# A GLA state update computed by pairs of sequences, two 64-row products side by side

## The chip, the cores and the metric

The kernel runs on one core of one Trainium2 chip. A core has a matrix engine (PE, with its weight loads listed apart as PEld), a vector engine (DVE), a scalar engine (ACT), a general engine (POOL) and an engine that mostly issues transfers (SP). They run their own instruction streams in order and wait for one another by semaphores. The metric is the device time of one execution in microseconds; lower is better.

## The reference

One step of a decoder layer: a Mamba-2 (SSD) branch and a gated linear attention (GLA) branch, merged by gates, then cross-attention and a convolutional feed-forward block, for a prompt of 256 tokens and, with the same weights, for 8 sample sequences of 4 tokens each. The change touches the sample part of the GLA branch, which has 4 heads with keys of 256 and values of 512:

```python
def step(S, inp):                       # here a chunk is the 4 tokens of a sample
    qc, kc, vc, gc = inp
    b = jnp.cumsum(gc, axis=1)
    qe = qc * jnp.exp(b)
    ke = kc * jnp.exp(-b)
    att = jnp.where(mask, jnp.einsum('bihk,bjhk->bhij', qe, ke), 0.0)
    o = jnp.einsum('bhij,bjhv->bihv', att, vc) + jnp.einsum('bihk,bhkv->bihv', qe, S)
    last = b[:, -1]
    S = jnp.exp(last)[..., None] * S + jnp.einsum('bjhk,bjhv->bhkv', kc * jnp.exp(last[:, None] - b), vc)
    return S, o
```

For each of 8 sequences and 4 heads, a state S of 256 x 512 floats is read from memory, used for the output, decayed, given a product of 4 tokens' keys and values, and written back.

## The kernel before

Everything is laid out with features on the 128 partitions and the 288 tokens (256 of the prompt, 32 of the samples) along the free axis. The bulk is projections (`proj_w`): a weight tile is loaded, split into a rounded high part (`whi`, ACT, L103) and the remainder (`wlo`, DVE, L105), and multiplied as high x high (L147), high x low (L148) and low x high (L151), 288 columns a matmul, in the format fp32r. The split tiles live in rings of five (`WB`). The products of the `mem` projections (L315, L316, L319) are the same with 512 columns.

Scans are generators that are woven into the projections: `weave` runs the projections of the next unit and the output projection of the last one as the main stream, and advances the scan by a share at each step. A `yield` is one such share, and `yield 1.25` counts as more. The final order on each engine is made by a scheduler that simulates a timeline; transfers marked `keep_in_program_order` keep their order. Four SSD units are followed by four GLA units, one for each head.

In a GLA unit (`gla_scan`, L1035) the 32 sample tokens are repeated four times down the partitions (`rep4`, L639), so that rows 0-31, 32-63, 64-95 and 96-127 hold the same tokens. `stack_r` (L646) gives the four groups of rows of `vst` the values' high, low, high, low parts, and `stack_l` (L657) gives `kst` and `atsl` the keys' high, high, low, low parts. One 128-row product of the two thus sums all four combinations, which restores nearly full precision.

The states come four ahead through POOL's queue (`load_state`, L1040), into six buffers of the tag `c4`. Then, for each half q of the sequences: eight products of queries and states for the output (L1150), each 32 columns wide, so that four of them lie in different column strips of the array; then for each sequence b a copy of `kst` masked to b's rows (`kb`, L1156), two products of 128 rows x 512 columns (L1159), each into its own bank of the three that `mm_tile` has, and two updates of the state on DVE (L1160). The state is stored through SP's queue (L1163), which also carries the weights, and the load of b + 4 follows.

The loop as it is before:

```python
for b in range(4 * q, 4 * q + 4):
    sin = sins[b]
    kb = pa.tile([P, 256], F32R, tag="kb", bufs=2, name="kb")
    V.tensor_scalar(kb, kst, bmask[:, b:b + 1], None, ALU.mult)
    for k in range(2):
        a = mm_tile()
        MM(a, kb[:, k * P:(k + 1) * P], vst, start=True, stop=True)
        V.scalar_tensor_tensor(sin[:, k, :], ...)
        yield 1.25
```

Other places named below: L566 is a small product of 32 rows in the set-up of the SSD branch; L870 is a product of the SSD scan that is 32 columns wide; L821, L823 and L825 are SSD products 64 columns wide; L398 and L469 are small DVE operations of the set-up.

Of the kernel before, what the change touches and what calls it, by code (L numbers as in the profile page):

```python
# [8 lines left out]
F32 = mybir.dt.float32  # L9
F32R = mybir.dt.float32r  # L10
# [6 lines left out]
P = 128  # L17
# [3 lines left out]
NB = 8  # L21
# [21 lines left out]
def hybrid_step(ctx: ExitStack, tc: tile.TileContext, I: dict, O: list):  # L43
# [185 lines left out]
    smask4 = p1.tile([P, NS], F32, name="smask4")  # L229
    smaski = p1.tile([P, NS], I32, name="smaski")  # L230
    bmask = p1.tile([P, NB], F32, name="bmask")
    rm_g = p1.tile([P, T], F32, name="rm_g")

    def starts(rm, c):
# [31 lines left out]
    with pool("p0") as p0:  # L266
# [194 lines left out]
        for c in range(4):  # L461
# [7 lines left out]
        V.tensor_copy(smaski, smask4)  # L469
# [169 lines left out]
    def rep4(src, name):  # L639
# [3 lines left out]
        V.tensor_copy(o, src.unsqueeze(2).to_broadcast([P, n, 4, NS]))  # L643
        return o.rearrange("p t r s -> p t (r s)")

    def stack_r(dst, src):  # L646

        S.copy(dst, src)
        for q in (1, 3):
            rows = slice(q * NS, (q + 1) * NS)  # L650
            V.tensor_tensor(dst[rows], src[rows], dst[rows], ALU.subtract)

    def own(a, q):

        return bass.AP(a.tensor, a.offset + 16 * q, [list(a.ap[0]), [P, 4], [NS + NL, 4], [1, NL]])

    def stack_l(dst, src):  # L657

# [376 lines left out]
    def gla_scan(h, eb, qe, ke, kd, kde, vT, sr):  # L1035

        sq = pa.tile([P, T], F32, tag="sq", bufs=1, name="sqa")
        sins = []

        def load_state(b):  # L1040
            sin = c4([P, 2, 512], "sin")
            tc.keep_in_program_order(G.dma_start(out=sin, in_=I["state_gla"][b, h].rearrange("(k p) v -> p k v", p=P)))
            sins.append(sin)
# [9 lines left out]
        vsr = rep4(vT[:, :, SEQ:T], "vsr")  # L1053
        ksr = rep4(kd[:, :, SEQ:T], "ksr")
        ker = rep4(ke[:, :, SEQ:T], "ker")

        vt = []
        for i in range(2):
            a = mm_tile()
            for t in range(4):  # L1060
                TR(a[:, t * P:(t + 1) * P], vT[:, t, i * P:(i + 1) * P], ident)
            v = b2("vt")
            S.copy(v, a)
            vt.append(v)
            yield

        a = mm_tile()
        for i, (t0, n) in enumerate(TOK):
            for k in range(2):
                MM(a[:, t0:t0 + n], ke[:, k, t0:t0 + n] if i < 2 else ker[:, k, :], qe[:, k, t0:t0 + n],  # L1070
                   start=(k == 0), stop=(k == 1))
        for i in range(2):
            for k in range(2):
                MM(a[:, 288 + 64 * i:352 + 64 * i], kd[:, k, P * i:P * i + P], qe[:, k, P * i + 64:P * i + P],
                   start=(k == 0), stop=(k == 1))
        V.copy_predicated(att, gmask.unsqueeze(1).to_broadcast([P, 2, P]),
                          a[:, 0:SEQ].rearrange("p (c n) -> p c n", n=P))
        V.copy_predicated(ats, smaski, a[:, SEQ:T])
        for rows, op in ((slice(0, P), None), (slice(2 * NS, P), ALU.subtract)):
            f, g = atsl[rows], ats[rows].rearrange("p (q j l) -> p q j l", j=4, l=NL)  # L1080
            f = bass.AP(f.tensor, f.offset, [list(f.ap[0]), [16, 2], [NS + NL, 4], [1, NL]])
            if op is None:
                S.copy(f, g)
            else:
                V.tensor_tensor(f, g, f, op)
        S.copy(att[0:64, :, 64:P], a[0:64, 288:416].rearrange("p (c n) -> p c n", n=64))
        for i in range(2):
            for k in range(2):
                V.tensor_copy(kd[:, k, P * i:P * i + 64], kde[:, k, i, :])
        yield  # L1090

        kt = b2("kt").rearrange("p (c k) -> p c k", k=256)
        a = mm_tile()
        for i in range(2):
            for k in range(2):
                TR(a[:, i * 256 + k * P:i * 256 + (k + 1) * P], kd[:, k, i * P:(i + 1) * P], ident)
        S.copy(kt.rearrange("p c k -> p (c k)"), a)
        yield
        a = mm_tile()
        for t in range(4):  # L1100
            TR(a[:, t * P:(t + 1) * P], vsr[:, t, :], ident)
        vst = r2("vst")
        stack_r(vst, a)
        yield
        a = mm_tile()
        for k in range(2):
            TR(a[:, k * P:(k + 1) * P], ksr[:, k, :], ident)
        kst = pa.tile([P, 256], F32R, tag="kst", bufs=1, name="kst")
        stack_l(kst, a[:, 0:256])
        for k in range(2):  # L1110
            diag(qdm[:, k], qe[:, k, SEQ:T])
        yield

        elp = pa.tile([P, 2], F32, tag="elp", bufs=1, name="elp")
        V.tensor_tensor(elp, eb[:, :, 191], eb[:, :, 255], ALU.mult)
        for k in range(2):
            V.tensor_scalar(qe[:, k, 192:256], qe[:, k, 192:256], eb[:, k, 191:192], None, ALU.mult)
        sprev = None
        for i in range(2):
            sn = c4([P, 2, 512], "sn")  # L1120
            for k in range(2):
                a = mm_tile()
                MM(a, kt[:, i, k * P:(k + 1) * P], vt[i], start=True, stop=True)  # L1123
                if i == 0:
                    S.copy(sn[:, k, :], a)
                else:
                    V.scalar_tensor_tensor(sn[:, k, :], sprev[:, k, :], elp[:, k:k + 1], a, ALU.mult, ALU.add)
                yield
            o = mm_tile()
            for t in range(4):  # L1130
                MM(o[:, t * P:(t + 1) * P], vt[i][:, t * P:(t + 1) * P], att[:, i, :], start=True, stop=(i == 0))
                if i == 1:
                    for k in range(2):
                        MM(o[:, t * P:(t + 1) * P], sprev[:, k, t * P:(t + 1) * P], qe[:, k, P:SEQ], start=False,
                           stop=(k == 1))
            evac(o, i * P, P)
            yield
            sprev = sn
        nc.sync.dma_start(out=o_pgla[0, h].rearrange("(k p) v -> p k v", p=P), in_=sprev)
        for b in range(4):  # L1140
            load_state(b)
        yield

        osa = la_tile()
        MM(osa, atsl, vst, start=True, stop=False)
        for q in range(2):
            for k in (1, 0):
                for j in (3, 2, 1, 0):
                    b = 4 * q + j
                    MM(osa[NS * j:NS * j + NS, :], qdm[:, k, b, :], sins[b][:, k, :], start=False,  # L1150
                       stop=(q == 1 and k == 0))
            yield
            for b in range(4 * q, 4 * q + 4):
                sin = sins[b]
                kb = pa.tile([P, 256], F32R, tag="kb", bufs=2, name="kb")
                V.tensor_scalar(kb, kst, bmask[:, b:b + 1], None, ALU.mult)  # L1156
                for k in range(2):
                    a = mm_tile()
                    MM(a, kb[:, k * P:(k + 1) * P], vst, start=True, stop=True)  # L1159
                    V.scalar_tensor_tensor(sin[:, k, :], sin[:, k, :], eb[:, k, SEQ + 4 * b + 3:SEQ + 4 * b + 4], a,  # L1160
                                           ALU.mult, ALU.add)
                    yield 1.25
                nc.sync.dma_start(out=o_sgla[b, h].rearrange("(k p) v -> p k v", p=P), in_=sin)  # L1163
                if b + 4 < NB:
                    load_state(b + 4)
            if h == 3 and q == 0:
                yield 3
        os_ = b2("os")
        S.copy(os_, osa)
        yield  # L1170
        a = mm_tile()
        for t in range(4):
            TR(a[:, t * P:(t + 1) * P], os_[:, t * P:(t + 1) * P], ident)
        ot = pa.tile([P, P], F32, tag="cst", bufs=2, name="ot")
        for q in range(2):
            S.copy(ot.rearrange("p (t q j l) -> p q t j l", t=4, q=2, j=4)[:, q], own(a, q))
        evac(ot, SEQ, NS)
        yield
        yield
        yield from finish(sr, sq, rg, False)  # L1180
# [650 lines left out]
```

## Time and profile before

| | us |
|---|---|
| median of 3 runs | 2519.35 |
| lowest and highest | 2517.22, 2526.04 |
| the profiled execution, its own time | 2522.44 |
| its span, first to last instruction | 2520.7 |
| state products L1159, first to last start | 771.6 to 1163.7 |

The page's second part shows the span in 40 slices. PE stands at 9 tenths or more nearly throughout, the granted clock at 9 or more in every slice, and the DMA engines between 5 and 8 tenths:

```profile
PE   9999999999999999999999999999999999999998
DVE  6656777796867666666666677567777677676765
PEclk9999999999999999999999999999999999999999
DMA  8776587767868675867778599655555555555553
```

A row of a timeline gives the start in us, the length in us, the engine, the line of the kernel, the operation, the tiles (out<-in), for PE the part of the array that the instruction uses (rows*columns, 128*128 being all of it), the shape and the count. A matmul's length is modelled and overlaps that of the next; its start is recorded. One fp32 matmul shows as two records (two passes), one fp32r matmul as one.

### The profile page before, as it was taken

The numbers are of one execution on the slowest core, as the hardware profiler recorded it, in microseconds if no ns is written. First come the engines' busy times: TensorE is split into PE (matmuls) and PEld (weight loads), VectorE is DVE, ScalarE is ACT, GpSimd is POOL, SyncE is SP. The second block draws the span as 40 slices with busy tenths as digits, with TensorE's granted clock in tenths as the row PEclk, the third lists the DMA queues.
The fourth block names the chain that finished last, engine by engine and source line by source line (L and its number), as shares of the span: only waits on it lengthen the run. The fifth ranks groups of instructions, "written<-read, shape, count | busy, mean of one in ns | idle before, by whom it ended". The sixth has DMA issues, their size and how long they took to land.

```text
span 2520.7 us, 50431 instructions
## 1 busy us (share of the span) xinstructions
PE 2502.4 (99%) x18914; PEld 2411.9 (96%) x18914; DVE 1753.1 (70%) x3752; ACT 1346.9 (53%) x2736; POOL 392.8 (16%) x729
## 2 busy tenths in 40 slices
PE   9999999999999999999999999999999999999998
PEld 8889999998999999999999989999999999999998
DVE  6656777796867666666666677567777677676765
ACT  7655647655463655454445544555555455454545
POOL 3002133342300010000001122402111001020010
PEclk9999999999999999999999999999999999999999
DMA  8776587767868675867778599655555555555553
GB/s 268 221 218 196 171 251 210 228 196 210 245 188 275 183 251 175 248 207 263 202 224 267 180 327 323 213 159 178 170 171 173 170 168 171 170 175 169 168 171 129
DMA packets 442021, 521.95 MB, mean 207 GB/s; under 512 B 26876, under 2 KB 390236, under 8 KB 441712
## 3 DMA queue, kind: packets, MB, share of 16 engines
q1 hardware_dynamic: 407728, 422.34, 54.3%
q0 software_dynamic: 34016, 96.38, 12.0%
q8 instruction: 148, 2.42, 0.4%
q14 instruction: 97, 0.79, 0.1%
q10 hardware_dynamic: 32, 0.01, 0.0%
HBM read 473.13 MB, written 45.48 MB: 206 GB/s over the span
## 4 chain that ended last, share of the span: by engine, by line
PE 95%; DMA 2%; DVE 1%; ACT 1%; issue 0%; POOL 0%; DVEq 0%; ACTq 0%; POOLq 0%
PE acc L148 27%; PE acc L147 27%; PE acc L151 26%; PE acc L315 2%; PE acc L316 2%; PE acc L319 2%; PE la L1541 1%; PE mm L1159 1%; PE la L1150 1%; DMA sqr<-in_state_ssd_dram 1%; PE la L1483 1%; PE mm L1123 1%; DMA sin<-in_state_ssd_dram 1%; DMA raw<-in_w_gla_out_dram 0%; POOL sqr L731 0%
## 5 line engine op out<-in xcount | busy, mean ns | idle before, releaser
L103 ACT CAST whi<-raw 128x512 fp32r<-128x512 f32 x1464 | 897.3, 618 | 1011.9 <-PE acc L148 783.6
L105 DVE TENSOR_TENSOR wlo<-raw,whi 128x512 fp32r<-128x512 f32 x1464 | 997.2, 687 | 607.9 <-ACT whi L103 590.5
L147 PE MATMUL acc<-xn,whi 128*128 128x288 f32 (+1 forms) x1936 | 550.2, 299 | 0.0
L148 PE MATMUL acc<-xn,whi 128*128 128x288 f32 (+1 forms) x1936 | 542.0, 296 | 0.0
L151 PE MATMUL acc<-xn,wlo 128*128 128x288 f32 (+1 forms) x1936 | 414.3, 295 | 0.0
L148 PE MATMUL acc<-hf,whi 128*128 128x288 f32 x1408 | 393.2, 295 | 0.0
L147 PE MATMUL acc<-hf,whi 128*128 128x288 f32 x1408 | 389.0, 292 | 0.0
L147 PEld LDWEIGHTS acc<-xn,whi 128*128 128x128 f32 (+1 forms) x1936 | 364.4, 188 | 9.9 <-issue 7.5
L148 PEld LDWEIGHTS acc<-xn,whi 128*128 128x128 f32 (+1 forms) x1936 | 364.5, 188 | 6.6 <-issue 4.6
L151 PEld LDWEIGHTS acc<-xn,wlo 128*128 128x128 f32 (+1 forms) x1936 | 310.5, 188 | 1.6 <-issue 1.3
L151 PE MATMUL acc<-hf,wlo 128*128 128x288 f32 x1408 | 294.5, 290 | 0.0
L148 PEld LDWEIGHTS acc<-hf,whi 128*128 128x128 f32 x1408 | 264.5, 188 | 0.1
L147 PEld LDWEIGHTS acc<-hf,whi 128*128 128x128 f32 x1408 | 264.0, 188 | 0.1
L151 PEld LDWEIGHTS acc<-hf,wlo 128*128 128x128 f32 x1408 | 226.3, 188 | 0.0
L148 PE MATMUL acc<-pr,whi 128*128 128x288 f32 x704 | 196.6, 295 | 0.0
L147 PE MATMUL acc<-pr,whi 128*128 128x288 f32 x704 | 195.0, 293 | 0.0
L151 PE MATMUL acc<-pr,wlo 128*128 128x288 f32 x704 | 147.4, 290 | 0.0
L147 PE MATMUL acc<-un,whi 128*128 128x288 f32 x512 | 145.3, 300 | 1.2 <-DVE mb L961 0.8
L148 PE MATMUL acc<-un,whi 128*128 128x288 f32 x512 | 143.0, 295 | 0.0
L1655 POOL COPY fsp<-fst 128x16 f32<-128x16 f32 x88 | 37.1, 424 | 656.5 <-DVE av L1667 422.0
L148 PEld LDWEIGHTS acc<-pr,whi 128*128 128x128 f32 x704 | 132.3, 188 | 0.0
L147 PEld LDWEIGHTS acc<-pr,whi 128*128 128x128 f32 x704 | 132.0, 188 | 0.0
(516 smaller groups left out, 4283.4 us busy)
## 6 DMA issues: line engine op xcount, KB each, us to landing
raw<-in_w_in_dram SPq DMA_DIRECT2D x240, 512.0 KB
raw<-in_w_up_dram SPq DMA_DIRECT2D x176, 512.0 KB
raw<-in_w_down_dram SPq DMA_DIRECT2D x88, 512.0 KB
raw<-in_w_cv_dram SPq DMA_DIRECT2D x32, 512.0 KB
raw<-in_w_ssd_out_dram SPq DMA_DIRECT2D x32, 512.0 KB
sin<-in_state_gla_dram POOLq DMA_DIRECT2D x32, 512.0 KB, 5.6
out_dram<-sin SPq DMA_DIRECT2D x32, 512.0 KB
raw<-in_w_gla_out_dram SPq DMA_DIRECT2D x32, 512.0 KB
```

What stands on the lines that cost most here:

```text
L103: S.copy(hi, raw)
L105: V.tensor_tensor(lo, raw, hi, ALU.subtract)
L147: MM(a, hi[:, k, cs], xh, start=(k0 + s0 + k == 0), stop=False)
L148: MM(a, hi[:, k, cs], xl, start=False, stop=False)
L151: MM(a, lo[:, k, cs], xh, start=False, stop=(k0 + s0 + k == nk - 1))
L315: MM(accs[m], mn_hi[:, kk, ms_], hi[:, 0, :], start=(kk == 0), stop=False)
L316: MM(accs[m], mn_lo[:, kk, ms_], hi[:, 0, :], start=False, stop=False)
L319: MM(accs[m], mn_hi[:, kk, ms_], lo[:, 0, :], start=False, stop=(kk == KT - 1))
L1123: MM(a, kt[:, i, k * P:(k + 1) * P], vt[i], start=True, stop=True)
L1150: MM(osa[NS * j:NS * j + NS, :], qdm[:, k, b, :], sins[b][:, k, :], start=False, stop=(q == 1 and k == 0))
L1159: MM(a, kb[:, k * P:(k + 1) * P], vst, start=True, stop=True)
L1655: G.tensor_copy(sp[:, :, 0:2], st.rearrange("p (b k) -> p b k", k=2))
```

## The change

Sequences are handled in pairs (b, b + 4). The rows of the repeated tokens are regrouped by halves: partitions 0-63 hold the 16 tokens of sequences 0-3 four times, partitions 64-127 those of sequences 4-7 (`rep16`, two copies in place of one). High and low parts are made over all rows at once: `stack` computes sign x source on ACT and low x source - that on DVE, with columns `signs` and `lows` of per-row constants (+1 and 1 where the row is to hold the low part, -1 and 0 where the high part). In the set-up these constants and a mask for pairs (`bpair`) are derived from a matrix `sub`, made by two operations on POOL and reduced on DVE.

The masked keys `kb` are made once for a pair. Each of the two sequences takes one half of the rows: two products of 64 rows x 512 columns, the first on partitions 0-63 and the second on 64-127, into two banks. The array fields of these instructions are 64*128, at rows 0 and 64. Then both states are updated. States are loaded in the order 0, 4, 1, 5, 2, 6, 3, 7; both states of a pair are stored together, and the next two loads follow.

```diff
+    def rep16(src, name):
+        n = src.shape[1]
+        o = b2(name).rearrange("p (t f r s) -> p f t r s", f=2, r=4, s=16)[:, :, 0:n]
+        for f in range(2):
+            V.tensor_copy(o[:, f], src[:, :, 16 * f:16 * f + 16].unsqueeze(2).to_broadcast([P, n, 4, 16]))
+        return o.rearrange("p f t r s -> p t f (r s)")
+
+    def stack(dst, src, w):
+        S.activation(dst, src, ACT.Identity, scale=signs[:, w:w + 1])
+        V.scalar_tensor_tensor(dst, src, lows[:, w:w + 1], dst, ALU.mult, ALU.subtract)
...
-        for rows, op in ((slice(0, P), None), (slice(2 * NS, P), ALU.subtract)):
...
+        atp = pa.tile([P, NS], F32R, tag="atp", bufs=1, name="atp")
+        stack(atp, ats, 1)
+        for f in range(2):
+            S.copy(bass.AP(atsl.tensor, atsl.offset + 80 * f, ...), atp[:, 16 * f:16 * f + 16]...)
...
-        stack_r(vst, a)
+        stack(vst, a, 0)
...
-        stack_l(kst, a[:, 0:256])
+        stack(kst, a[:, 0:256], 1)
...
-        for b in range(4):
+        for b in (0, 4, 1, 5):
             load_state(b)
...
-                    b = 4 * q + j
+                    b = 4 * (j // 2) + 2 * q + j % 2
                     MM(osa[NS * j:NS * j + NS, :], qdm[:, k, b, :], sins[b][:, k, :], start=False,
...
-            for b in range(4 * q, 4 * q + 4):
-                sin = sins[b]
+            for j in (2 * q, 2 * q + 1):
                 kb = pa.tile([P, 256], F32R, tag="kb", bufs=2, name="kb")
-                V.tensor_scalar(kb, kst, bmask[:, b:b + 1], None, ALU.mult)
+                V.tensor_scalar(kb, kst, bpair[:, j:j + 1], None, ALU.mult)
                 for k in range(2):
-                    a = mm_tile()
-                    MM(a, kb[:, k * P:(k + 1) * P], vst, start=True, stop=True)
-                    V.scalar_tensor_tensor(sin[:, k, :], sin[:, k, :], eb[...], a, ALU.mult, ALU.add)
-                    yield 1.25
-                nc.sync.dma_start(out=o_sgla[b, h]..., in_=sin)
-                if b + 4 < NB:
-                    load_state(b + 4)
+                    au = [mm_tile() for _ in range(2)]
+                    for f in range(2):
+                        rows = slice(64 * f, 64 * f + 64)
+                        MM(au[f], kb[rows, k * P:(k + 1) * P], vst[rows], start=True, stop=True)
+                    for f in range(2):
+                        b, sin = j + 4 * f, sins[j + 4 * f]
+                        V.scalar_tensor_tensor(sin[:, k, :], sin[:, k, :], eb[...], au[f], ALU.mult, ALU.add)
+                    yield 2.5
+                for b in (j, j + 4):
+                    nc.sync.dma_start(out=o_sgla[b, h]..., in_=sins[b])
+                    if j + 2 < 4:
+                        load_state(b + 2)
...
-        for q in range(2):
-            S.copy(ot...[:, q], own(a, q))
+        for f in range(2):
+            for q in range(2):
+                S.copy(ot...[:, f, q], own2(a, f, q))
```

More of the change, by code (lines that the diff above doesn't have):

```diff
@@ L231, in hybrid_step @@
     bmask = p1.tile([P, NB], F32, name="bmask")
+    half_ = p1.tile([P, 8], F32, name="half_")
+    bpair, lows, signs = half_[:, 0:4], half_[:, 4:6], half_[:, 6:8]
     rm_g = p1.tile([P, T], F32, name="rm_g")
@@ L468, in hybrid_step @@
                             channel_multiplier=-1)
-        V.tensor_copy(smaski, smask4)
+        sub = p0.tile([P, NS, NL], F32, name="sub")
+        G.affine_select(sub, ones.rearrange("p (x l) -> p x l", l=NL), pattern=[[4, NS], [1, NL]], compare_op=ALU.is_ge,
+                        fill=0.0, base=0, channel_multiplier=-1)
+        G.affine_select(sub, sub, pattern=[[-4, NS], [0, NL]], compare_op=ALU.is_ge, fill=0.0, base=0, channel_multiplier=1)
+        smg = p0.tile([P, 2, 16], F32, name="smg")
+        V.tensor_reduce(smg, sub.rearrange("p (f r j) l -> p f (j l) r", f=2, r=4), axis=AX.X, op=ALU.add)
+        V.tensor_copy(smaski, smg.rearrange("p f x -> p (f x)"))
+        last = smg.rearrange("p f (j l) -> p f j l", l=NL)[:, :, :, NL - 1]
+        V.tensor_tensor(bpair, last[:, 0], last[:, 1], ALU.add)
+        own4 = sub[:, :, NL - 1]
+        odd = p0.tile([P, 4], F32, name="odd")
+        for w, v in enumerate((own4.rearrange("p (a r j) -> p r a j", r=2, j=4)[:, 1],
+                               own4.rearrange("p (a r j) -> p r a j", r=2, j=8)[:, 1])):
+            V.tensor_reduce(odd[:, 0:v.shape[1]], v, axis=AX.X, op=ALU.add)
+            V.tensor_reduce(lows[:, w:w + 1], odd[:, 0:v.shape[1]], axis=AX.X, op=ALU.add)
+        V.tensor_scalar(signs, lows, 2.0, -1.0, ALU.mult, ALU.add)
         gm_f = p0.tile([P, P], F32, name="gm_f")
```

35 lines of the change are left out of this document (16 added, 19 removed).

## The prediction

> **What bounds the kernel now.** I read the page first, busy times and the chain that ended last.
>
> ```profile
> PE 2502.4 (99%) x18914; PEld 2411.9 (96%) x18914; DVE 1753.1 (70%) x3752; ACT 1346.9 (53%) x2736; POOL 392.8 (16%) x729
> PE 95%; DMA 2%; DVE 1%; ACT 1%; issue 0%; POOL 0%; DVEq 0%; ACTq 0%; POOLq 0%
> ```
>
> PE, the matrix engine, sets the time. A busy PE says little here, since ends of matmuls are modelled; so from here on I use starts only, and the distance from one start to the next. The changed code runs inside the four GLA scans, between 724 and 1182 us. Busy time of each engine in that stretch, and the chain cut to it:
>
> ```profile
> 724.00:1182.00 458.00, 458.00 (x3401) 433.76 (x3401) 306.34 (x610) 233.43 (x420) 31.77 (x49) 1.00 0.72 226
> by line: PE acc L148 27.1%; PE acc L147 27.1%; PE acc L151 26.7%; PE mm L1159 3.3%; PE la L1150 3.2%; PE mm L1123 3.0%; PE mm L1134 1.6%; PE mm L1131 1.6%; PE mm L1070 1.1%; PE mm L1074 0.8%; PE mm L1061 0.8%; issue 0.5%; PE mm L1096 0.4%;
> ```
>
> Columns of the first row: the stretch, its length, busy us of PE, PEld (weight loads), DVE, ACT, POOL, granted clock, DMA share, GB/s. The clock is full, DVE works 67% and ACT 51%, and hardly anything but matmuls is on the chain. So the change is worth what it does to PE's own sequence; the state product (L1159) holds 3.3% of 458 us, 15.1 us over 64 products, 0.236 us each.
>
> **What one state product costs now.** The group, then PE's order of work around one product, then the same neighbours without one:
>
> ```profile
> L1159 PE MATMUL mm<-vst,kb x64: 389/398/403, 771.6 to 1163.7; 128*128 128x512 f32 x64
> ...
> 771.29 0.43 PE L151 MATMUL acc<-un,wlo 128*128 128x288 f32 x2
> 771.55 0.40 PE L1159 MATMUL mm<-vst,kb 128*128 128x512 f32 x1
> 771.79 0.30 PE L147 MATMUL acc<-un,whi 128*128 128x288 f32 x1
> 771.93 0.30 PE L148 MATMUL acc<-un,whi 128*128 128x288 f32 x1
> ...
> 768.93 0.42 PE L151 MATMUL acc<-un,wlo 128*128 128x288 f32 x2
> 769.18 0.29 PE L147 MATMUL acc<-un,whi 128*128 128x288 f32 x1
> 769.31 0.29 PE L148 MATMUL acc<-un,whi 128*128 128x288 f32 x1
> ```
>
> From the L151 pair to L148 it is 0.64 us with a product and 0.38 without: 0.26. The chain gives 0.236. I take 0.25 us a product, **0.50 for two**. Note the field 128*128: all of these use the array undivided.
>
> **What the change puts in its place.** Two products of 64 rows each, field 64*128, into two PSUM banks. The trace has no such form. It has others that divide the array, and they show the same thing at their edges. Nearest is L566, divided by rows (32*128), between undivided 512-column products; PE first, then its weight loads:
>
> ```profile
> 153.64 0.40 PE L315 MATMUL acc<-whi,mn_hi 128*128 128x512 f32 x1
> 153.87 0.39 PE L316 MATMUL acc<-whi,mn_lo 128*128 128x512 f32 x1
> 154.10 0.63 PE L319 MATMUL acc<-wlo,mn_hi 128*128 128x512 f32 x2
> 154.66 0.48 PE L566 MATMUL mm<-elm,hsel 32*128 32x128 f32 x2
> 155.07 0.50 PE L315 MATMUL acc<-whi,mn_hi 128*128 128x512 f32 x1
> 155.41 0.39 PE L316 MATMUL acc<-whi,mn_lo 128*128 128x512 f32 x1
> ...
> 154.66 0.29 PEld L566 LDWEIGHTS mm<-elm,hsel 32*128 32x128 f32 x2 [0.37 <-PE acc L316]
> 155.07 0.19 PEld L315 LDWEIGHTS acc<-whi,mn_hi 128*128 128x128 f32 x1
> 155.18 0.19 PEld L316 LDWEIGHTS acc<-whi,mn_lo 128*128 128x128 f32 x1
> ```
>
> Plain products follow each other in 0.23 (153.64, 153.87, 154.10). Entry: two L319 should take 0.46 and take 0.56, so 0.10 extra. Inside: 0.41 to the next L315, of which the two passes stream 2 x 0.107 (from the next fence). The other 0.20 is a weight load that hides behind nothing (0.11, as 155.07 to 155.18 shows for one of 128 columns) and 0.09 of emptying. Exit: L315 to L316 takes 0.34 instead of 0.23, another bare load, 0.11. Normally a load starts one matmul ahead; at a change of division it starts with its own matmul. Together **0.10 + 0.20 + 0.11 = 0.41 us for one island** in undivided work.
>
> The second form is four column strips: L1150, and L870 as a short island:
>
> ```profile
> 766.44 1.92 PE L1150 MATMUL la<-sin,qdm 128*32 128x512 f32 x16
> ...
> 766.89 0.13 PEld L1150 LDWEIGHTS la<-sin,qdm 128*32 128x32 f32 x4 [0.30 <-issue]
> 767.32 0.13 PEld L1150 LDWEIGHTS la<-sin,qdm 128*32 128x32 f32 x4 [0.30 <-issue]
> ...
> 363.05 0.41 PE L151 MATMUL acc<-xn,wlo 128*128 128x288 f32 x2
> 363.40 0.63 PE L870 MATMUL mm<-xds,mss 128*32 128x256 f32 x4
> 363.95 0.40 PE L147 MATMUL acc<-xn,whi 128*128 128x288 f32 x1
> 364.19 0.29 PE L148 MATMUL acc<-xn,whi 128*128 128x288 f32 x1
> ```
>
> L1150: sixteen 512-column passes of 0.59 in 1.92 us, four at a time, a round every 0.43 us (0.107 per 128 columns): different strips do run side by side. L870: 1.14 us over neighbours that take 0.38, so 0.76, less two rounds of 256 columns (0.43): 0.33, the same toll with loads of 32 columns for 128.
>
> Now the new island. Streaming 512 columns in fp32r lies between 0.215 (half the fp32 round) and 0.23 (plain spacing): 0.22. The second half starts 0.01 later (four loads within 0.13). So **a pair side by side costs 0.41 + 0.22 + 0.01 = 0.64 us against 0.50 before: +0.14**. A half that stands alone pays the whole toll: 0.63 against 0.25, +0.38. In the order in which the changed program is built, 27 of the 32 pairs are adjacent and 5 are torn apart (the last pair of the first three heads, two in the last head), with L147/L148/L151 between. Sum: 27 x 0.14 + 10 x 0.38 = 3.8 + 3.8 = **+7.6 us**.
>
> Bounds, since rows as strips beside each other are not in this trace: if the second load waits for the first, +0.11 per pair (27 x 0.11 = 3.0 more); if the second product streams only after the first, +0.22 per pair (5.9 more); if a division by 64 rows pays no toll, a pair costs 0.26, that is 27 x -0.24 = -6.5 and nothing for single halves. I take the toll because both divisions shown, by rows and by columns, pay it, and side by side because the column strips do.
>
> The row first: L566 loses 0.10 going in and 0.09 going out beside its bare loads. The Trainium skill, "TensorEngine Tiling (Array Packing)", Key Properties, says why: a change of tiling mode, not of tile alone, drains the engine. The trace agrees with it. The same page's Theoretical Speedup gives up to 2x for 64 rows; by that figure alone, without the drain, 32 pairs would save 32 x 0.24 = 7.7 us, and the change would pay.
>
> **The other edits, off PE's path.** DVE rows by shape for this stretch:
>
> ```profile
> L1160 DVE SCALAR_TENSOR_TENSOR sin<-sin,eb,mm 128x512 f32<-128x512 f32 x64 | 47.6, 745 | 27.3 <-PE mm L1159 26.7
> L1156 DVE TENSOR_SCALAR kb<-kst,bmask 128x256 fp32r<-128x256 f32 x32 | 10.8, 348 | 0.3
> L651 DVE TENSOR_TENSOR vst<-mm,vst 32x512 fp32r<-32x512 f32 x8 | 5.5, 690 | 0.6 <-ACT vst L648 0.3
> ```
>
> Per head DVE loses four masks (4 x 0.35) and two partial subtractions (2 x 0.69), and gains one full-height multiply-subtract of 512 (0.75, as L1160, also out of PSUM); a half-height one of 256 becomes a full-height one, and three repeats become six of half the size. That is 1 to 2 us a head less, on an engine 67% busy: 0. ACT gets four more small copies a head, on an engine 51% busy: 0. Two updates now come back to back, 1.5 us in which no wlo is made; PE holds five split weight tiles (WB) of twelve 0.13 us matmuls, 7.8 us. Without that cover it would cost 0.75 per pair. The set-up has two more POOL masks and seven more small DVE operations, which fall here:
>
> ```profile
> 30.93 0.16 DVE L398 TENSOR_REDUCE mrs<-mss 128x2 f32<-128x8 f32 x1 [0.88 <-ACT junk L347]
> 31.44 1.90 DVE L105 TENSOR_TENSOR wlo<-raw,whi 128x512 fp32r<-128x512 f32 x3 [0.35 <-ACT whi L103]
> ```
>
> At 0.16 each that is 1.1 us, into 1.23 us of idle time: 0, and at most 1.1 were they all in the way and the weight ring empty.
>
> The stores of b and b+4 now stand together, and the last two state loads on POOL's queue wait for both. PE's second group of L1150 waits for those loads, and everything on PE queues behind it. In the tightest head, the last, then in the first; then the last head's busy times, and the load's row of the page:
>
> ```profile
> 1130.30 0.38 SPq L1163 DMA_DIRECT2D out_dram<-sin  x1
> 1138.46 0.71 POOL L1042 DMA_DIRECT2D sin<-in_state_gla_dram  x1 [3.12 <-DVE wlo L105]
> 1146.52 1.92 PE L1150 MATMUL la<-sin,qdm 128*32 128x512 f32 x16
> ...
> 786.64 0.71 POOL L1042 DMA_DIRECT2D sin<-in_state_gla_dram  x1 [7.00 <-DVE kb L1156]
> 797.13 0.64 PE L1150 MATMUL la<-sin,qdm 128*32 128x512 f32 x4
> ...
> 1121.00:1164.00 43.00, 43.00 (x318) 39.05 (x317) 33.38 (x61) 15.31 (x26) 3.40 (x5) 1.00 0.83 276
> sin<-in_state_gla_dram POOLq DMA_DIRECT2D x32, 512.0 KB, 5.6
> ```
>
> Store to load 8.2, load to landing 5.6, at 1144.1: 2.4 us spare; in the first head 797.13 - 786.64 - 5.6 = 4.9. The new stores come about 1 us later, PE itself about 1.5 later: 0.
>
> **Rivals.**
> 1. *The halves don't overlap fully* (loads or streams one after the other). For: no pair of row strips in this trace. Against: 0.43 a round for four column strips. +10.6 to +13.5: 2530.0 to 2532.9.
> 2. *No toll for 64 rows*, so the change wins; the other side. It decides if the entry into a pair is below about 0.03 and loads stay ahead. For: nothing but that 64 rows are not 32. Against: L566 and L870 both pay. -6.5: 2512.9.
> 3. *The toll and a new wait*: the joint stores make the last two loads late. For: two 512 KB loads at once with 83% of DMA time taken in the last head. Against: 2.4 and 4.9 us spare. At 2 us in up to four heads: 2529 to 2535.
> 4. *It doesn't do what it says*: pairs torn apart. Known for 5; were all 32, 64 x 0.38 = +24.3, 2543.7; the built order excludes it.
>
> **Numbers.** The profiled execution took 2522.44 us (span 2520.7 and 1.7 around it), 3.1 above the median of the three runs, 2519.35. Forecast: 2522.44 + 7.6 - 3.1 = **2527.0 us**. Chances: forecast 0.55, rival 1 0.22, rival 2 0.10, rival 3 0.08, anything else 0.05. The forecast's own range is 2523 to 2531 (0.02 us of reading on each term, and runs 2517 to 2526). Rival 2's centre and the top of rival 3 stay outside: range 2515 to 2534. About 0.3%, 7.6 us, is what a measurement can tell from no change; the forecast sits on that line. Slower by more: half of the forecast (0.28), nearly all of 1 and 3 (0.28), 0.02 of the rest: 0.58. Faster by more: a third of rival 2 and a little else, 0.07. Within: 0.35.
>
> **What would show it.** Right: matmuls 64*128 with about 0.225 from the last L151 to the first of a pair, starts of a pair within 0.01, about 0.42 from the second to the next L147, and 0.24 from that L147 to L148; the whole stretch of scans 7 to 8 us longer. Starts 0.11 or 0.22 apart would mean rival 1; 0.13 and 0.24 around a pair rival 2; a gap ahead of L1150 rival 3. I'd be wrong altogether if PE waited for DVE or PSUM inside a pair.

## The result and the profile after

The changed kernel takes 2546.57 us (median of 4 runs, 2542.81 to 2550.82), the kernel before beside it 2518.28 (4 runs): a ratio of 1.0105, interval 1.0088 to 1.0123, or 26.4 us (the medians alone lie 28.3 apart). The forecast of 2527.0 was far too low, and the range ended at 2534.

The lines of the page that answer to those of before, and the stretch of the four GLA scans:

```profile
PE 2520.1 (99%) x18914; PEld 2412.9 (95%) x18914; DVE 1748.5 (69%) x3751; ACT 1348.1 (53%) x2752; POOL 393.4 (15%) x731
PE 93%; DMA 3%; DVE 1%; POOL 1%; ACT 1%; issue 0%; DVEq 0%; ACTq 0%; SPq 0%; POOLq 0%
...
740.00:1208.00 468.00, 468.00 (x3403) 431.66 (x3402) 300.60 (x600) 236.44 (x437) 31.74 (x49) 1.00 0.70 221
```

As many matmuls as before, and the clock in the scans is full as before. On the chain PE has 93% instead of 95%, DMA 3% instead of 2%.

The pairs of products first, where the forecast had looked. PE's order and its weight loads around the first pair of the first head, changed kernel (start, duration, engine, line; L1191 is the product, L147, L148, L151 as before):

```profile
787.57 0.43 PE L151 MATMUL acc<-un,wlo 128*128 128x288 f32 x2
787.92 0.19 PEld L1191 LDWEIGHTS mm<-vst,kb 64*128 64x128 f32 x2 [0.17 <-issue]
787.92 0.51 PE L1191 MATMUL mm<-vst,kb 64*128 64x512 f32 x2
788.36 0.19 PEld L147 LDWEIGHTS acc<-un,whi 128*128 128x128 f32 x1 [0.25 <-issue]
788.36 0.40 PE L147 MATMUL acc<-un,whi 128*128 128x288 f32 x1
788.60 0.29 PE L148 MATMUL acc<-un,whi 128*128 128x288 f32 x1
```

Both halves start at 787.92 and are done in 0.51 us. From the L151 pair to L148 it takes 1.03 us. So the pair behaves as forecast, and costs as much as forecast. The time went elsewhere. To see where, three marks are followed through the program: the memory projections (from first to last start), the first transposition of vT, which opens the first GLA scan, and the last transposition of os, which closes the last one. Each kernel's own line, minimum, median and maximum of one in ns, then first and last start in us; before, then after:

```profile
L315 PE MATMUL acc<-whi,mn_hi x256: 389/389/612, 7.4 to 200.5; 128*128 128x512 f32 x128
L1061 PE MATMUL mm<-ident,vT x32: 271/272/273, 724.8 to 1090.1; 128*128 128x128 f32 x32
L1173 PE MATMUL mm<-ident,os x16: 270/272/273, 829.5 to 1169.0; 128*128 128x128 f32 x16
```

```profile
L317 PE MATMUL acc<-whi,mn_hi x256: 389/396/610, 7.4 to 204.3; 128*128 128x512 f32 x128
L1094 PE MATMUL mm<-ident,vT x32: 270/272/273, 741.0 to 1113.3; 128*128 128x128 f32 x32
L1208 PE MATMUL mm<-ident,os x16: 271/272/273, 848.2 to 1195.0; 128*128 128x128 f32 x16
```

The changed kernel is 3.8 us late at the end of the memory projections (204.3 against 200.5), 16.2 when the first GLA scan begins (741.0 against 724.8) and 26.0 at the end of the last. The span is 25.7 longer (2546.4 against 2520.7), so nothing happens behind it. **Of 26 us, 16 are lost ahead of the first scan**, where the change edits nothing but masks in the set-up. Three things differ there.

First, the matmuls of the memory projections: the median of one is 396 ns instead of 389. From start to start the 768 of them take 5 ns more each (by the starts in the traces 233 and 238 ns on average, 227 and 233 in the median), 768 x 5 ns = 3.8 us.

Second, in the scans of SSD the transfers of POOL's queue take longer. Stretch 300 to 720 us before, 304 to 736 after: what ACT waited for ahead of the weight split (us in total, times, longest), and the issues (KB each, median us from issue to landing); before, then after:

```profile
ACT whi L103 <- DMA raw<-in_w_in_dram: 30.9, 18, 4.5
ACT whi L103 <- DMA raw<-in_w_ssd_out_dram: 10.5, 5, 3.4
...
sqr<-in_state_ssd_dram POOLq DMA_DIRECT2D x128, 64.0 KB, 5.2
sin<-in_state_ssd_dram POOLq DMA_DIRECT2D x32, 256.0 KB, 5.2
```

```profile
ACT whi L103 <- DMA raw<-in_w_in_dram: 58.2, 24, 7.4
ACT whi L103 <- DMA raw<-in_w_ssd_out_dram: 21.2, 8, 5.9
...
sqr<-in_state_ssd_dram POOLq DMA_DIRECT2D x128, 64.0 KB, 6.9
sin<-in_state_ssd_dram POOLq DMA_DIRECT2D x32, 256.0 KB, 7.0
```

The same transfers, as many and as large, land 1.7 us later, and ACT waits 38 us longer for weights (58.2 + 21.2 against 30.9 + 10.5). Most of that is covered by the split weight tiles in hand.

Third, where the cover ends, PE stops. The costliest place, where PE waits for a copy (cst) that stands behind the late weights in ACT's order; PE and ACT before, then after:

```profile
567.97 0.27 PE L601 MATMUL mm<-ident,cache 128*108 128x128 f32 x1
571.67 0.50 PE L894 MATMUL mm<-bblk,wst 128*128 128x256 f32 x2 [3.43 <-ACT cst L603]
...
570.31 1.14 ACT L103 CAST whi<-raw 128x512 fp32r<-128x512 f32 x2 [4.55 <-DMA raw<-in_w_in_dram]
571.36 0.26 ACT L603 COPY cst<-mm 108x128 f32<-108x128 f32 x1
```

```profile
577.41 0.27 PE L618 MATMUL mm<-ident,cache 128*108 128x128 f32 x1
584.93 0.80 PE L928 MATMUL mm<-bblk,wst 128*128 128x256 f32 x2 [7.25 <-ACT cst L620]
...
583.57 1.14 ACT L103 CAST whi<-raw 128x512 fp32r<-128x512 f32 x2 [5.37 <-DMA raw<-in_w_in_dram]
584.62 0.26 ACT L620 COPY cst<-mm 108x128 f32<-108x128 f32 x1
```

PE stands still for 7.25 us instead of 3.43, by 3.8 us more at this one place. Over the whole stretch from the memory projections to the first GLA scan, PE's idle time in the two traces adds up to 12.9 us instead of 4.5. Behind such stops the granted clock halves (last section): 8.0 us of PE's work fall on half the clock instead of 3.4, which is worth 2.3 us more. That makes 10.7 of the 12.4 us that are lost behind the projections (16.2 less 3.8).

What can reach work that was not edited? The diff has one line that touches all of it: the new tile half_, 32 bytes per partition, allocated ahead of rm_g. By the addresses in the built programs most tiles allocated behind it in the pools p1, p0 and pa lie 32 bytes higher, and those that also stand behind another new tile more (kst and kb 160, part of the set-up's tiles 704): mn_hi goes from 120832 (a multiple of 256) to 120864, sqr from 144000 (a multiple of 128) to 144032, sin from 182784 (a multiple of 256) to 182816. The tiles of raw, whi, wlo and xn lie in pools ahead of it and stay.

### The profile page after: what moved, and what is told of

It is laid out like the page before. It is cut to its first block, busy times and chain, and to the rows that moved or that the text cites. A ratio compares the mean times of both kernels' runs of the same rounds, so it can differ in the third digit from the quotient of the medians.

```text
span 2546.4 us, 50452 instructions
## 1 busy us (share of the span) xinstructions
PE 2520.1 (99%) x18914; PEld 2412.9 (95%) x18914; DVE 1748.5 (69%) x3751; ACT 1348.1 (53%) x2752; POOL 393.4 (15%) x731
## 3 DMA queue, kind: packets, MB, share of 16 engines
q0 software_dynamic: 34016, 96.38, 12.1%
## 4 chain that ended last, share of the span: by engine, by line
PE 93%; DMA 3%; DVE 1%; POOL 1%; ACT 1%; issue 0%; DVEq 0%; ACTq 0%; SPq 0%; POOLq 0%
PE acc L148 26%; PE acc L147 26%; PE acc L151 26%; PE acc L317 2%; PE acc L318 2%; PE acc L321 2%; DMA raw<-in_w_in_dram 1%; DMA sqr<-in_state_ssd_dram 1%; PE mm L1191 1%; PE la L1181 1%; PE la L1519 1%; PE mm L1154 1%; DMA raw<-in_w_co_dram 0%; PE la L1577 0%; DMA kc<-in_cache_mem_k_dram 0%
## 5 line engine op out<-in xcount | busy, mean ns | idle before, releaser
L147 PE MATMUL acc<-xn,whi 128*128 128x288 f32 (+1 forms) x1936 | 553.5, 301 | 2.6 <-ACT whi L103 1.7
L148 PE MATMUL acc<-xn,whi 128*128 128x288 f32 (+1 forms) x1936 | 541.8, 295 | 0.0
L151 PE MATMUL acc<-xn,wlo 128*128 128x288 f32 (+1 forms) x1936 | 415.2, 296 | 0.0
L148 PE MATMUL acc<-hf,whi 128*128 128x288 f32 x1408 | 393.1, 295 | 0.0
L147 PE MATMUL acc<-hf,whi 128*128 128x288 f32 x1408 | 389.0, 292 | 0.0
L147 PEld LDWEIGHTS acc<-xn,whi 128*128 128x128 f32 (+1 forms) x1936 | 364.5, 188 | 17.5 <-issue 12.0
L148 PEld LDWEIGHTS acc<-xn,whi 128*128 128x128 f32 (+1 forms) x1936 | 364.8, 188 | 4.9 <-issue 4.6
L151 PEld LDWEIGHTS acc<-xn,wlo 128*128 128x128 f32 (+1 forms) x1936 | 310.7, 188 | 2.8 <-issue 2.0
L151 PE MATMUL acc<-hf,wlo 128*128 128x288 f32 x1408 | 294.5, 290 | 0.0
L148 PEld LDWEIGHTS acc<-hf,whi 128*128 128x128 f32 x1408 | 264.5, 188 | 0.1
L147 PEld LDWEIGHTS acc<-hf,whi 128*128 128x128 f32 x1408 | 264.0, 188 | 0.1
L151 PEld LDWEIGHTS acc<-hf,wlo 128*128 128x128 f32 x1408 | 226.2, 188 | 0.0
L148 PE MATMUL acc<-pr,whi 128*128 128x288 f32 x704 | 196.5, 295 | 0.0
L147 PE MATMUL acc<-pr,whi 128*128 128x288 f32 x704 | 195.0, 293 | 0.0
L147 PE MATMUL acc<-un,whi 128*128 128x288 f32 x512 | 148.7, 306 | 2.6 <-DVE ma L995 2.6
L151 PE MATMUL acc<-pr,wlo 128*128 128x288 f32 x704 | 147.4, 290 | 0.0
L148 PE MATMUL acc<-un,whi 128*128 128x288 f32 x512 | 144.7, 297 | 0.0
L148 PEld LDWEIGHTS acc<-pr,whi 128*128 128x128 f32 x704 | 132.3, 188 | 0.0
L147 PEld LDWEIGHTS acc<-pr,whi 128*128 128x128 f32 x704 | 132.0, 188 | 0.0
```

The source lines that it names most:

```text
L147: MM(a, hi[:, k, cs], xh, start=(k0 + s0 + k == 0), stop=False)
L148: MM(a, hi[:, k, cs], xl, start=False, stop=False)
L151: MM(a, lo[:, k, cs], xh, start=False, stop=(k0 + s0 + k == nk - 1))
```

## The experiments

Each kernel's ratio stands against runs of the kernel before on the same chip; the us behind it are (ratio - 1) x 2521, about their median there. The experiments on the kernel before keep its instructions and their order; only addresses move. Offsets are in bytes per partition.

**The addresses, or the new instructions?** Four kernels. e1, the kernel before with a tile that nothing uses:

```diff
+    p1.tile([P, 8], F32, name="shift_")
     rm_g = p1.tile([P, T], F32, name="rm_g")
```

> The kernel before with one unused tile of 32 bytes per partition put ahead of rm_g, where the changed kernel has half_. No instruction is added or removed; every tile of the pools p1, p0 and pa that is allocated behind it sits 32 bytes higher, as in the changed kernel. Theory A (the part of the loss outside the scans comes from these addresses): 16 to 17 us longer than before, about 2535 (2532 to 2538); the 512-column matmuls of the memory projections follow each other in about 232 ns instead of 227, and the 4096-byte packets of POOL's queue in the SSD scans take about 228 ns instead of 180. Theory B (it comes from the added set-up instructions or the new order of work): 2518, packets and spacing as before.

2540.01 us, 1.0074 (1.0059 to 1.0089): 18.7 us longer. An unused tile alone brings as much as the changed kernel lost ahead of its scans.

```profile
L316 PE MATMUL acc<-whi,mn_hi x256: 389/396/610, 7.7 to 205.0; 128*128 128x512 f32 x128
```

The 396 ns are there too. A packet is what a transfer engine moves at a time; the median of the 4096-byte packets (here as below worked out from the packet records, 300 to 720 us) is 227 ns against 178. Theory B falls. e2, the changed kernel with `half_ = p1.tile([P, 16], ...)`, so that what half_ moves lies 64 bytes from its old place, not 32:

> The changed kernel with half_ made 64 bytes per partition instead of 32, nothing else: the tiles behind it are then again at multiples of 64 bytes where they were so before. Theory A (addresses): the loss ahead of the scans goes away and only the pairs' toll in the scans stays, 2526 to 2528. Theory B (set-up instructions, order): 2546 as the changed kernel.

2548.46, 1.0102 (1.0088 to 1.0116): no gain. Either the step that counts is larger than 64 bytes, or it isn't the address. e3, e2 with undivided products:

```diff
-MM(au[f], kb[rows, k * P:(k + 1) * P], vst[rows], start=True, stop=True)
+MM(au[f], kb[:, k * P:(k + 1) * P], vst, start=True, stop=True)
```

> As the run before it (half_ of 64 bytes), and each of the two products of a pair uses all 128 rows instead of its 64, so that the array is never divided there; every sample's state then gets the sum of the products of both sequences of its pair, which is not what the reference asks. Number of instructions, their order, tiles, stores and loads stay. Theory A (the scans' loss is the toll of divided products): 7 to 9 us under the run before, 2518 to 2520. Rival (the scans' loss is from the joint updates, stores and late loads): no change, 2526 to 2528.

2541.66, 1.0077 (1.0064 to 1.0089). The absolute times were missed, as e2 had already gone wrong, but a difference is there: 6.3 us under e2 by the ratios (6.8 by the medians), just short of the 7 to 9 expected: the toll of the division. e4, the kernel before with `bmask`, `acs`, `ss` and `elp` widened, so that nearly all stands at multiples of 64:

> The kernel before with four small tiles (bmask, acs, ss, elp) widened so that the tiles behind them that were at 32 past a multiple of 64 bytes (mp, xf, xr, dg among them) also start at a multiple of 64; no instruction changes. If addresses set the price of every tile alike: 2 to 6 us faster than before, 2512 to 2516. If only some tiles matter (those of the state loads and of the memory projections, which are aligned in the kernel before already): 2518, the same.

2539.06, 1.0067 (1.0053 to 1.008): 17 us *longer*, which neither side expected. The widened tiles moved mn_hi, sqr and sin by 64 as in e2. The kernel before lies on places that 64 is too coarse to describe.

**Which step, which tiles?** f1 widens `bmask` by 128 bytes:

> The kernel before with bmask widened by 128 bytes per partition: the order of the work stays and every tile behind it moves by 128 bytes. Theory C (a tile must keep its place modulo 128 bytes: the moves by 32 and 64 bytes both cost 16 us): 2518 to 2523, spacing of the 512-column matmuls 227 ns, median of the 4096-byte packets in the scans of SSD 175 to 180 ns. Rival D (any other place is worse, for instance by a larger period or by how the tiles lie to those that don't move): 2535 to 2541.

2525.24, 1.0015 (1.0004 to 1.0025): 3.8 us longer instead of 17. So 128 restores most of it, but all three signs were missed: the time lies 2 us above its range, the memory projections stay slow (232 ns from start to start), and the packets stay at 225 ns.

```profile
L315 PE MATMUL acc<-whi,mn_hi x256: 389/393/607, 8.0 to 204.0; 128*128 128x512 f32 x128
```

f2 sets only mn_hi and mn_lo off by 32:

```diff
+        p0.tile([P, 8], F32, name="pad_a")
         mn_hi = p0.tile([P, KT, SEQ], F32R, name="mn_hi")
         mn_lo = p0.tile([P, KT, SEQ], F32R, name="mn_lo")
+        p0.tile([P, 24], F32, name="pad_b")
```

> The kernel before with 32 unused bytes ahead of mn_hi and 96 behind mn_lo: these two tiles, from which the memory projections load their weights into PE, are 32 bytes off a multiple of 128, the rest of their pool moves by 128 bytes, all other tiles stay. Theory C with the loss in the memory projections put down to these two: 4 to 5 us longer, 2523 to 2527, spacing 232 ns instead of 227, nothing lost in the scans of SSD. Rival (the loss there comes from other tiles, or from DMA): no change.

2526.16, 1.0011 (1.0 to 1.0022), 2.8 us; in the trace 3.7 at the end of the projections (204.3 - 7.5 against 200.5 - 7.4):

```profile
L317 PE MATMUL acc<-whi,mn_hi x256: 389/396/607, 7.5 to 204.3; 128*128 128x512 f32 x128
```

The loss in the projections is that of PE's weight reads from these two tiles. f3 takes `[:, 8:520]` instead of `[:, 0:512]` of sqr's tile:

> The kernel before with the 512 values of sqr placed 32 bytes further inside their own tile, which has room for 576; no tile moves. sqr takes the sample states of SSD in pieces of 128 bytes. Theory C with the loss in SSD put down to these transfers: 10 to 12 us longer, 2529 to 2534, median of the 4096-byte packets of POOL's queue 178 to 228 ns and of sqr's transfers 4.6 to 6.8 us. Rival (the loss in SSD comes from other tiles): 2519 to 2523 with packets as before.

2527.01, 1.0018 (1.0008 to 1.0029): 4.5 us, less than half of what was expected, and a packet median of 181, though the transfers of sqr land after 6.5 us:

```profile
ACT whi L103 <- DMA raw<-in_w_in_dram: 55.7, 26, 5.2
ACT whi L103 <- DMA raw<-in_w_ssd_out_dram: 12.6, 7, 5.0
...
sqr<-in_state_ssd_dram POOLq DMA_DIRECT2D x128, 64.0 KB, 6.5
sin<-in_state_ssd_dram POOLq DMA_DIRECT2D x32, 256.0 KB, 6.3
```

f4 is the changed kernel without half_; its eight values fill the unused bytes behind two small tiles:

```diff
-    dtb = const.tile([32, 1], F32, name="dtb")
-    alog = const.tile([32, 1], F32, name="alog")
+    dtb_ = const.tile([P, 8], F32, name="dtb")
+    dtb, bpair = dtb_[0:32, 0:1], dtb_[:, 4:8]
+    alog_ = const.tile([P, 8], F32, name="alog")
+    alog, lows, signs = alog_[0:32, 0:1], alog_[:, 4:6], alog_[:, 6:8]
...
-    half_ = p1.tile([P, 8], F32, name="half_")
-    bpair, lows, signs = half_[:, 0:4], half_[:, 4:6], half_[:, 6:8]
```

> The changed kernel without the tile half_: its eight values lie in the unused bytes behind dtb and alog, so that every large tile has its address of before. Theory C: only the pairs' toll is left, 7 to 10 us over before, 2527 to 2531. Rival (the added set-up work costs something besides the address): 2535 or more.

**2528.6, 1.0033 (1.0019 to 1.0046): 8.3 us over before**, where 7.6 were forecast. All of the change is in it, but for the place of eight numbers.

**The rest of the SSD loss.** h2 puts 32 unused bytes ahead of the six buffers of sin and 96 behind them; h3 does this and also moves sqr and ab (`[:, :, 8:264]`) within their tiles; h5 does it to the small tiles from rm_g to qdm; h1 moves the weight ring instead.

> The kernel before with 32 unused bytes ahead of the six buffers of sin and 96 behind them; r2, un, kde, kst and kb move by 128, all other tiles stay. sin takes sample states in pieces of 512 bytes. If a transfer's place modulo 128 bytes is what counts, for these pieces as for the 128-byte pieces of sqr: 3 to 6 us longer, 2524 to 2528, and the 4096-byte packets of the SSD scans at 180 to 228 ns. Rival (pieces of 512 bytes don't care): 2519 to 2523.

2523.53, 1.001 (1.0001 to 1.0019), 2.5 us, just short of the 3 to 6 expected. The packets' median is 225, and in f3 it was 181: it is sin's place that this median shows.

> As the run before it, and sqr and ab placed 32 bytes further inside their own tiles, so that every tile which POOL's queue fills in the scans of SSD is 32 bytes off. If these three make the loss in the scans of SSD (12 to 14 us of the 18 that the shift by 32 cost): 11 to 15 us longer, 2532 to 2537. Rival (most of it comes from tiles that only engines touch): 2525 to 2529.

2533.21, 1.0048 (1.0036 to 1.0061), 12.1 us, as expected. Its rows for 300 to 720 us read like those of the changed kernel:

```profile
ACT whi L103 <- DMA raw<-in_w_in_dram: 53.8, 23, 6.4
ACT whi L103 <- DMA raw<-in_w_ssd_out_dram: 19.3, 8, 5.7
...
sqr<-in_state_ssd_dram POOLq DMA_DIRECT2D x128, 64.0 KB, 6.7
sin<-in_state_ssd_dram POOLq DMA_DIRECT2D x32, 256.0 KB, 6.9
```

> The kernel before with 32 unused bytes ahead of rm_g and 96 behind qdm: the small tiles that live through the scans (rm_g to qdm) are 32 bytes off, the tiles of the two pools behind them move by 128. If the loss comes from what transfers fill and from PE's weights in the memory projections alone, this costs what the move by 128 cost, 2523 to 2527. Rival (tokc, scst, att, qdm and the like matter for the engines that read them): 2530 or more.

2526.79, 1.0024 (1.0015 to 1.0032): 6 us, inside its expectation. In f1, too, the tiles behind move by 128, and it cost 3.8; the intervals of the two overlap, so a loss of the small tiles themselves, some 2 us, is not shown.

> The kernel before with smask4 and smaski (128 bytes each) moved ahead of the weight ring, so that raw, whi, wlo, xn, h and all tiles of the later stages move by 256 bytes, from 256 past a multiple of 512 to a multiple; everything from bmask on keeps its address. In the memory projections the weights of PE (mn_hi, mn_lo) lie at multiples of 512 and a matmul takes 227 ns; moved by 32, by 64 or by 128 it takes 232 to 234. If every weight load that isn't at a multiple of 512 pays so, the projections with whi and wlo as weights (some 15,700 matmuls of 288 columns, 130 to 133 ns apart) pay now, and gain 3 to 6 ns each: 47 to 94 us shorter, about 2430 to 2475. Rival (a place at 256 past a multiple of 512 is as good, or these are bound by their columns): 2519 to 2524.

2521.47, 1.0007 (0.9995 to 1.0019): nothing won. Spacing of the 288-column matmuls stays at 130 to 133 ns. A place at 256 past a multiple of 512 is as good as one at 512.

**Closing the account.** i1 sets mn_hi and mn_lo 256 bytes further, i2 is h3 and f2 together, i3 is f4 with undivided products.

> The kernel before with mn_hi and mn_lo 256 bytes past a multiple of 512 (256 unused bytes ahead of them and 256 behind; the rest of their pool moves by 512). If the weight reads of PE need a multiple of 256: 227 ns between 512-column matmuls, 2519 to 2523. If they need a multiple of 512: 232 to 233 ns, 2523 to 2527.

2519.59, 0.9999 (0.9987 to 1.001): 256 it is.

```profile
L317 PE MATMUL acc<-whi,mn_hi x256: 387/390/612, 7.2 to 201.3; 128*128 128x512 f32 x128
```

> The kernel before with mn_hi, mn_lo, sqr, ab and the buffers of sin 32 bytes off their places, the rest of the tiles at their places or moved by 128. If these five are the whole loss of the shift by 32: 16 to 19 us longer, 2536 to 2540. Rival (the rest of the tiles hold a share): 2531 to 2535.

2537.27, 1.007 (1.0058 to 1.0083), 17.6 us: the five tiles hold the whole loss of the unused tile (18.7).

> The changed kernel without half_ (its values behind dtb and alog, addresses as before), and both products of a pair with all 128 rows, so that the array is undivided there; every sample's state then gets the sum of the products of both sequences of its pair. Toll theory: all but 1 to 2 us of the loss is gone, 2520 to 2524. Rival (joint updates, stores and late loads cost by themselves): 2527 to 2530.

2519.76, 1.0002 (0.9993 to 1.0011), by the ratios 7.8 us under f4: the division of the array is all that the change itself costs.

```profile
768.78 0.43 PE L153 MATMUL acc<-un,wlo 128*128 128x288 f32 x2
769.04 0.63 PE L1191 MATMUL mm<-vst,kb 128*128 128x512 f32 x2
769.51 0.30 PE L149 MATMUL acc<-un,whi 128*128 128x288 f32 x1
769.65 0.29 PE L150 MATMUL acc<-un,whi 128*128 128x288 f32 x1
```

Two whole products take 0.87 us from the L153 pair to L150, where the divided pair took 1.03. Last, ab alone: k1 moves it by 32, k2 lays its two rows back to back so that both start at a multiple of 256.

> The kernel before with only ab 32 bytes further inside its own tile. ab takes pieces of 1024 bytes, twelve transfers of 256 KB in the SSD scans. If the loss of the three tiles adds up: 4 us longer, 2523 to 2526. Rival (the pieces of ab are too long to mind, and the three lose more together than each alone because they share the transfer engines): 2518 to 2522.

2521.08, 1.0001 (0.9988 to 1.0013): nothing. So the three lose more together (12.1) than each alone (4.5, 2.5 and 0).

> The kernel before with the two rows of ab back to back, 128 bytes into its tile, so that both start at a multiple of 256 bytes instead of one of two. If 256 is the step that counts and the transfers of the SSD scans bound the weights there: 1 to 3 us shorter, 2516 to 2519. Rival: 2519 to 2522, the same.

2522.66, 1.0003 (0.999 to 1.0015): the same. No version tried beats the kernel before; f4 is the best form of the change that computes the right states.

## Why the prediction was wrong

**One product before, 0.25 us**: right. Over all places with these neighbours the distance from the first L151 to L148 has a median of 0.635 us with a product and 0.394 without, 0.24.

**The island, 0.64 us**: right. Over the 27 adjacent pairs the same distance has a median of 1.029, less 0.394: 0.635. The parts agree as well: 0.225 from the last L151 to the pair, 0.43 from its second half to L147 (0.42 forecast), 0.24 on to L148 (medians; 788.60 - 788.36 in the fence above). Rival 1 (halves one after the other) and rival 2 (no toll) are out. The one torn half with these neighbours: 1.011 - 0.394 = 0.62 instead of 0.63. All 10 torn halves and 27 pairs stood where the built order had them.

**The sum of the scans, +7.6**: right to about 1 us by the runs. With the measured distances, 27 x (1.029 - 0.394 - 2 x 0.241) + 10 x (1.011 - 0.394 - 0.241) = 4.1 + 3.8 = 7.9, where the 1.011 of one torn half stands for all ten; the runs give 6.3 (e2 less e3) and 7.8 (f4 less i3), the profiled execution 9.8 (26.0 - 16.2).

**Joint stores, late loads, DVE and ACT edits, 0**: right within the interval. i3 has all of them and no toll, and takes 1.0002 of the time before. Rival 3 is out.

**The set-up, "0, and at most 1.1"**: this step failed. It priced the added instructions, and those indeed cost nothing (f4), but not the tile that they write to. half_ is part of the diff; the list of what the change adds left it out, so neither its 32 bytes nor the tiles behind it got a term. It is worth about 18 us, more than twice the term on which the forecast was built: e1 18.7, i2 17.6, the changed kernel less f4 18.1. No rival had it either, and so the range, made of doubts about the pair alone, ended 12.6 us short.

How a place costs time is shown as far as this: with mn_hi and mn_lo, the weights, at 32, 64 or 128 past a multiple of 256 (f2, e2, f1) the matmuls start 5 to 7 ns further apart (medians 227 against 232 to 234), and no further at 256 (i1); sqr, filled in pieces of 128 bytes, lands late at 32 past a multiple of 128 (f3, where it moved alone, 6.5 us against 5.2) and, moved with the rest, at 64 (e2, 6.8); sin, filled in pieces of 512, has slower packets at 32 and at 128 past a multiple of 256. sqr and sin come by the same queue, and one delays the other: in f3 sin, at its old place, lands after 6.3 us instead of 5.2, and ACT's wait for weights grows from 41.4 to 68.3 us. PE pays where no split weights are left. The Trainium skill, "DMA: Bandwidth & Descriptors", section How a descriptor splits into AXI transactions, has a rule that fits the transfers: a piece becomes transactions that each start at a multiple of 256 bytes, so that what crosses such a multiple is split there. The page tells it of what a transaction reads; that it holds for SBUF as the target, too, is assumed here. By it every second piece of sqr is split in two at 32 or 64 but none at 128, and a piece of sin goes from two parts to three at 32, 64 and 128 alike. The traces agree: f1, at 128, has slow packets of sin (225 ns) but sqr landing after 5.6 us, as in f4 with sqr at its old place, not after 6.5 to 6.9. That PE's reads follow the same step of 256 is only seen, not explained.

Still open: why sqr, sin and ab together cost 12.1 where 4.5 + 2.5 + 0 are accounted for. Waits that are covered one by one and not together would do it, and the traces, one execution each, point that way: between 300 and 745 us PE is idle for 10.0 us in h3, against 4.5 in the kernel before, 6.7 in f3, 2.9 in h2 and 6.6 in k1; and h3 runs at half the clock for 10.2 us, against 3.4 in the kernel before, f3 and h2 and 6.8 in k1. f1, with mn_hi, mn_lo and sin off their places but not sqr, costs no more (3.8) than these alone (2.8 and 2.5), so the excess seems to need sqr. A run with sqr and sin alone was not tried. f1's profiled execution loses 2.9 us in the memory projections (204.0 - 8.0 against 200.5 - 7.4); where the rest of its 3.8 lies was not settled.

## What to carry to other kernels

A new tile is an edit to every tile allocated behind it. Before a change is priced, list the tiles that it adds, see by how much those behind them move, and look at which of them are weights of PE or the target of transfers in short pieces; put the new tile in bytes that lie unused (f4), or last, or round it up to 256 (these two were not run). When a loss shows up ahead of the edited code, try the addresses before the instructions: one unused tile settles it.

A short run of products on part of the array costs some 0.4 us here for changing over and back, beside what it streams: about 0.41 for the pairs (0.635 less 0.22), 0.41 for L566 and 0.33 for L870 by the prediction's working. So it should pay only where many stand together, which no run here tried.

## What was unexpected of the hardware

After a wait of PE the granted clock halves, and not during the wait alone. The stop that was shown above, in single microseconds with others between them left out (length, busy us of PE, PEld, DVE, ACT, POOL, granted clock, DMA share, GB/s); before (PE idle 568.2 to 571.7), then after (577.7 to 584.9):

```profile
570.00:571.00 1.00, 0.00 (x0) 0.00 (x0) 0.04 (x1) 0.69 (x2) 0.65 (x1) 1.00 1.02 299
572.00:573.00 1.00, 1.00 (x8) 1.00 (x7) 0.62 (x2) 0.00 (x0) 0.90 (x3) 0.76 1.13 337
574.00:575.00 1.00, 1.00 (x6) 1.00 (x6) 0.65 (x2) 0.32 (x1) 0.00 (x0) 0.50 0.98 195
577.00:578.00 1.00, 1.00 (x10) 1.00 (x9) 0.74 (x2) 0.01 (x1) 0.00 (x0) 1.00 0.98 326
```

```profile
582.00:583.00 1.00, 0.00 (x0) 0.00 (x0) 0.00 (x0) 0.00 (x0) 0.63 (x1) 0.82 1.08 159
586.00:587.00 1.00, 1.00 (x6) 1.00 (x6) 0.37 (x1) 0.60 (x1) 0.00 (x0) 0.50 0.77 187
590.00:591.00 1.00, 1.00 (x9) 1.00 (x9) 0.20 (x1) 0.62 (x1) 0.00 (x0) 1.00 0.91 320
```

At 0.50 PE starts 6 matmuls in a microsecond instead of 9 or 10, so a stop costs more than its length. The clock falls within the microsecond from 572 before and from 582 after, 4 to 5 us after the stop began (in k1 it fell after 2.0 us, at 571.0 in a stop from 569.0). In the kernel before PE had gone on at 571.7, so there all of the slow time falls on work. By the clock's records it lasts 3.41 us before and 6.83 us after; the changed kernel has another 3.41 us of it from 671.4, behind a stop of 2.18 us.

The Trainium skill, "TensorE: Matmul & The Clock Gate", section What's actually happening, puts half rate behind an idle window of about 3.4 us. The stop of 3.43 us fits that, but shorter ones were enough in other runs, 2.64 us in f4 and 2.08 in h5 (below, the stop and the clock behind it), while after 2.39 us in k2 the clock stayed at 1.00. So in this case a stop of 2.1 us can already bring the half rate, and why one of 2.39 us did not is open.

```profile
575.08 0.50 PE L896 MATMUL mm<-bblk,wst 128*128 128x256 f32 x2 [2.08 <-ACT cst L605]
...
577.00:578.00 1.00, 1.00 (x6) 1.00 (x5) 0.00 (x0) 0.45 (x1) 0.32 (x1) 0.50 1.10 311
```

The other surprise is the main one: 32 bytes of unused memory cost 18.7 us of 2521, and 128 bytes 3.8.
